# Gates of tiles 6 and 7 as seven block products, with attention's last steps between them

## The chip, the core and the metric

The kernel runs on one core of a Trainium2 chip. The metric is device time in microseconds, the median of several executions. The core has five engines with a queue each: TensorE (PE) multiplies, VectorE (DVE) and ScalarE (ACT) do element-wise work, GpSimd (POOL) does a little element-wise work here, and SyncE (SP) issues the DMAs. Each queue runs in program order; the queues meet only where one waits for another's result or for a buffer.

## What is computed

One decoder block on 512 tokens of width 1024, in float32. Its core, cut down:

```python
u = modulate(rmsnorm(h, g_norm_ffn1), sh1, sc1)
h = h + 0.5 * gt1 * swiglu(u, w_ffn1_in, w_ffn1_out)
u = modulate(rmsnorm(h, g_norm_mix), sh2, sc2)
proj = u @ w_in                       # p | q | k | v | gate_logits
y_pool = multiscale_pool(p, w_pool, pool_scale)
# rotary q, k; three groups of heads, dilations 1, 4, 16; groups joined by their softmax denominators
y_attn = einsum('gbsh,gbshd->bshd', softmax(lses), outs)
g_pool, g_attn = split(sigmoid(gate_logits), 2)
merged = g_pool * (y_pool @ w_pool_branch) + g_attn * (y_attn @ w_attn_branch)
h = h + gt2 * (merged @ w_out)
u = modulate(rmsnorm(h, g_norm_ffn2), sh3, sc3)
h = h + 0.5 * gt3 * swiglu(u, w_ffn2_in, w_ffn2_out)
return rmsnorm(h, g_final)
```

The nine modulation vectors (sh1 to gt3) are products of silu(c) with a 1024 x 9216 matrix, 72 rows of 128 results.

## The kernel before

Activations lie transposed, 128 features on the partitions and 512 tokens along them; a feature tile is 128 features, so there are 8 of them. Every float32 factor is split in a high and a low part (fp32r), and a product is three matmuls: high by high, high by low, low by high.

**Weights.** `plan` (L176) writes down the order in which PE consumes weights: `order` has one entry for each piece of 1024 columns, with the raw loads that it needs and, for block products, the sum that makes it. `fetch` issues loads from SP into three raw buffers as they come free. `split_hi` (ACT) and `split_lo` (DVE) write the high and low parts into a ring of 6784 columns; `make` (DVE, L313) forms a sum of raw blocks first where an entry asks for one. `look(n)` splits up to n entries ahead of the one PE is at, as far as the ring has room; `take` hands the parts to PE.

**Plain tiles and block products.** `mm_tile` computes one feature tile of `u @ w` with 8 x 3 matmuls of 512 columns. `gate_duo` (L1774) computes two gates of two feature tiles (four tiles' worth) by seven block products instead of eight: both factors are cut in 2 x 2 blocks, seven products of sums of blocks are formed, and the results are added. `product` (L741) is one of them, 24 matmuls of 256 columns. A `settle` matmul of 240 columns, whose result is overwritten, stands ahead of the first. The seven products need four sums of blocks of the weights (`make`) and four of u (`mix_sums`, L1310: each is formed on DVE and then split on ACT and DVE).

**The stage around the change.** `mix` (L1602) computes q, k, v and p, rope, and three attention groups. Attention is cut into units whose steps are hung between matmuls of other tiles as hooks at k = 0 to 7: `at_scores` (PE), `at_exp` (DVE, ACT), `at_turn` (PE transpose, ACT copy), `at_values` (PE, DVE copy). The loop over c = 0 to 3 (L1740) computes v of the two dilated groups for one class of tokens at a time; it needs a copy of u's high part sorted by class, which `by_class` (L1706, an ACT instruction) makes one pass ahead. Beside it run steps of `mix_sums` (`nxt`), the four weight pieces of v are all held in the ring, and POOL forms the pooling differences (`pool_diff`, L1560). Then come four plain gate tiles (L1756 to L1768, feature tiles 6 and 7, two gates each) with attention's last steps hung between them: the last `at_values`, `at_merge` (small DVE and ACT steps that weigh the groups), `pool_map`, `at_fT`, `at_spread` (PE) and `at_y` (DVE). `merge_out` (L1814) follows: the two branch products of tiles 6 and 7 with those gates, then three times a `gate_duo` and two branches, then the output product.

The background step `bg` (L466) computes one modulation row: a 512 KB load by SP and a 1024-wide DVE instruction (L449). Rows 45 to 59 belong to this stage.

Of the kernel before, what the change touches and what calls it, by code (L numbers as in the profile page):

```python
# [14 lines left out]
P = 128  # L15
# [146 lines left out]
def chunk_widths():  # L162
    outs = [D] * (KT // 2 * (len(PARTS) - 1)) + [(FT - PARTS[-1][0]) * P] * KT
    f1 = [2 * FIRST * P] * KT + [D] * (2 * (FT - FIRST)), outs
    mix = [D] * 24 + [4 * P] * 2 + ([D] * 4 + [4 * P] * 2) * (KT // 2 - 1) + [D] * KT
    return f1, mix, ([D] * (2 * FT), outs)


class Kernel:
# [6 lines left out]
    def plan(self):  # L176
# [1133 lines left out]
    def mix_sums(self, x, slots):  # L1310
# [13 lines left out]
        def lo(i):  # L1324
            L[i] = slots[i][1]()
            v.tensor_tensor(L[i], x[i], H[i], op=OP.subtract)

        sub = lambda o, y, z: v.tensor_tensor(o, y, z, op=OP.subtract)

        def last():  # L1330
# [3 lines left out]
            self.S[:3] = [[H[i], L[i]] for i in range(3)]  # L1334
# [4 lines left out]
                lambda: (hi(0), whole(x[3], 4, 0)), lambda: lo(0), lambda: (hi(1), sub(x[3], x[3], x[1])),  # L1339
                lambda: hi(2), lambda: lo(2), lambda: lo(1)], last  # L1340
# [219 lines left out]
    def pool_diff(self, t, bank):  # L1560
# [6 lines left out]
        d = self.kt[0][:, T * t:T * t + T]  # L1567
# [34 lines left out]
    def mix(self):  # L1602
# [12 lines left out]
        with tc.tile_pool(name="rt", bufs=1) as self.rt, tc.tile_pool(name="aw", bufs=2) as self.aw, \  # L1615
# [23 lines left out]
            self.ada_free, self.ada_stop, self.ada_depth = list(x), 57, 2  # L1639
# [15 lines left out]
            for n in range(4):  # L1655
# [15 lines left out]
                for _ in range((0, 0, 1, 2)[n]):  # L1671
# [42 lines left out]
            assert self.ada_next == 57 and not self.adat, self.ada_next  # L1714
            self.ada_free, self.ada_stop, self.ada_depth = [self.AR], 60, 1
            self.bg_fetch()
            v4 = []

            def half(i):
                if not v4:  # L1720
# [4 lines left out]
                                       [wide(ma, "v1"), wide(ma, "k0")], [lambda: half(0), lambda: half(1)]])  # L1725
            nxt = lambda: sums.pop(0)()
            b = self.mm_tile(hooks(g23[0], [(2, lambda: by_class(1)), (3, nxt)]))
# [4 lines left out]
            def clear():  # L1732
# [5 lines left out]
            beside = [(1, 7, nxt), (2, 2, nxt), (2, 3, clear), (2, 6, self.bg), (2, 7, nxt), (3, 2, self.at_swap), (3, 2, nxt),  # L1738
                      (3, 3, nxt), (3, 6, nxt), (3, 7, self.bg)]
# [19 lines left out]
            rest = [b for b in self.banks if b not in gates] + [self.bS[0]]  # L1759
            spread = [self.bS[1], self.bO] + self.bT  # L1760
            self.banks, self.bi = gates + rest + spread, 2

            at = [t[:, i * T:(i + 1) * T] for t in (self.qt[1], self.kt[1]) for i in range(2)]
            sig = lambda i: lambda: nc.scalar.activation(at[i], gates[i], AF.Sigmoid)
            gates.append(self.mm_tile({1: [nxt, sig(0)], 2: [sig(1)], 4: [lambda: self.at_spread(spread)]}))
            self.YH, self.YL = two("YH"), two("YL")
            self.at_y(spread)
            gates.append(self.mm_tile({1: [sig(2)]}))  # L1768
            sig(3)()
            assert not sums  # L1770
        self.merge_out(at, last, ma)
        outer.close()

    def gate_duo(self, s, c, p5, last, rest):  # L1774
# [11 lines left out]
        for i, (bank, u, start) in enumerate(((A, lambda: blk(lo4, T1), True), (B, lambda: S(0), True),  # L1786
# [8 lines left out]
            self.product(bank, u(), start, not i)  # L1795
# [13 lines left out]
            elif i == 6:  # L1809
                sig(q(s, 1), r(A))  # L1810
                v.tensor_tensor(q(c, 0), r(B), q(c, 0), op=OP.add)
        sig(c, c)

    def merge_out(self, ready, last, ma):  # L1814
        nc, tc = self.nc, self.tc
        v = nc.vector
        with tc.tile_pool(name="mg", bufs=1) as mg:
# [15 lines left out]
            def branch(m):  # L1833
# [16 lines left out]
                def parts():  # L1850
                    if m > 5:
                        place(tile_of(ma, ("q1", "k1")[m % 2]), m)
# [9 lines left out]
            for j in MERGED[::2]:  # L1862
# [6 lines left out]
                for m in (j, j + 1):  # L1869
                    if m < 4:  # L1870
                        place(tile_of(*((ma, "q0"), (ma, "o1"), (mg, "m3"), (ma, "q2"))[m]), m)
# [281 lines left out]
```

## Time and profile before

| what | value |
|---|---|
| median of 3 runs | 971.73 us (970.31 to 972.13) |
| profiled execution, own time | 970.52 us |
| its span | 968.7 us |
| PE, DVE, ACT, POOL busy | 99%, 88%, 56%, 8% |
| granted TensorE clock | 0.998 |
| loop over the classes of v, first to last matmul of 512 columns | 449.42 to 482.60 us |
| four plain gate tiles | 482.60 to 509.22 us |

The span lies inside the profiled execution's own time. Times in rows below are from the span's start. In a row of the timeline the first two numbers are start and duration; what stands in brackets is the idle time of the engine before it and who ended it. A row with "x2" holds two instructions. PE's durations overlap: a matmul lasts longer than the distance to the next one, and the distance is what it costs.

### The profile page before, as it was taken

To read this page: it belongs to the slowest core of one execution; us is meant where nothing else is said; L and a number is where in the kernel's file an instruction comes from. 1 tells how busy PE (TensorE), PEld (TensorE's weight loads), DVE (VectorE), ACT (ScalarE), POOL (GpSimd) and SP (SyncE) were. 2 spreads that over 40 slices of the span, in tenths; PEclk is the share of its full clock that TensorE was granted. 3 is DMA by queue.
4 is the path that set the end of the run, shared out by engine and by line. 5 is a ranking of instruction groups with operands and counts; after the bars stand their busy time and mean duration, and the time that the engine had idled before them with its cause. 6 is when DMAs were issued, how large, how long until landed. Compare 5 with 4: busy or idle time off the path is not lost.

```text
span 968.7 us, 17985 instructions
## 1 busy us (share of the span) xinstructions
PE 958.6 (99%) x7222; PEld 899.6 (93%) x7222; DVE 847.8 (88%) x1250; ACT 542.1 (56%) x823; POOL 72.9 (8%) x81
## 2 busy tenths in 40 slices
PE   8999999999999999999999999999999999999997
PEld 7888999999999899888879998998999999999996
DVE  7989999899999788897888877889898888989885
ACT  5443656665755553446545553465665747566555
POOL 0000110101010000006300000000101100110002
PEclk9999999999999999999999999999999999999999
DMA  9857786786768547664143327723757666665632
GB/s 349 287 174 261 192 238 161 197 217 153 204 185 260 163 145 209 225 194 157 40 137 112 107 66 238 242 68 113 189 147 192 163 171 169 161 171 137 172 76 88
DMA packets 51702, 167.81 MB, mean 173 GB/s; under 512 B 6945, under 2 KB 9761, under 8 KB 51618
## 3 DMA queue, kind: packets, MB, share of 16 engines
q1 hardware_dynamic: 43840, 140.18, 44.3%
q0 software_dynamic: 7200, 25.96, 14.9%
q8 instruction: 56, 0.92, 0.4%
q10 hardware_dynamic: 578, 0.53, 0.2%
q14 instruction: 28, 0.23, 0.1%
HBM read 135.29 MB, written 2.24 MB: 142 GB/s over the span
## 4 chain that ended last, share of the span: by engine, by line
PE 95%; DVE 2%; DMA 1%; issue 1%; POOL 0%; ACT 0%; SPq 0%; POOLq 0%; DVEq 0%
PE bank L751 13%; PE bank L750 13%; PE bank L752 13%; PE bank L422 10%; PE bank L424 10%; PE bank L423 10%; PE bank L1109 5%; PE bank L1110 5%; PE bank L1111 5%; PE bank L2079 2%; PE bank L2083 1%; PE bank L2081 1%; PE bank L1451 1%; PE bank L1748 1%; PE bank L1502 1%; PE bank L1749 1%
## 5 line engine op out<-in xcount | busy, mean ns | idle before, releaser
L390 DVE TENSOR_TENSOR wlo<-raw,whi 128x1024 fp32r<-128x1024 f32 (+6 forms) x157 | 166.7, 1074 | 33.0 <-ACT whi L378 32.7
L750 PE MATMUL bank<-UH,whi 128*128 128x256 f32 x640 | 176.7, 276 | 0.0
L751 PE MATMUL bank<-UL,whi 128*128 128x256 f32 x640 | 176.7, 276 | 0.0
L752 PE MATMUL bank<-UH,wlo 128*128 128x256 f32 x640 | 176.7, 276 | 0.0
L390 DVE TENSOR_TENSOR wlo<-X,whi 128x1024 fp32r<-128x1024 f32 (+6 forms) x140 | 142.8, 1034 | 17.5 <-ACT whi L378 17.4
L378 ACT ACTIVATE whi<-raw 128x1024 fp32r<-128x1024 f32 (+6 forms) x157 | 144.0, 934 | 23.9 <-DVE raw L313 10.4
L378 ACT ACTIVATE whi<-X 128x1024 fp32r<-128x1024 f32 (+6 forms) x140 | 123.7, 908 | 49.5 <-DVE X L313 45.5
L750 PEld LDWEIGHTS bank<-UH,whi 128*128 128x128 f32 x640 | 120.1, 188 | 0.2
L751 PEld LDWEIGHTS bank<-UL,whi 128*128 128x128 f32 x640 | 120.2, 188 | 0.0
L752 PEld LDWEIGHTS bank<-UH,wlo 128*128 128x128 f32 x640 | 120.2, 188 | 0.0
L750 PE MATMUL bank<-SH,whi 128*128 128x256 f32 x408 | 112.7, 276 | 0.0
L751 PE MATMUL bank<-SL,whi 128*128 128x256 f32 x408 | 112.6, 276 | 0.0
L752 PE MATMUL bank<-SH,wlo 128*128 128x256 f32 x408 | 112.6, 276 | 0.0
L422 PE MATMUL bank<-UH,whi 128*128 128x512 f32 (+1 forms) x304 | 105.9, 348 | 0.0
L423 PE MATMUL bank<-UL,whi 128*128 128x512 f32 (+1 forms) x304 | 104.5, 344 | 0.1
L424 PE MATMUL bank<-UH,wlo 128*128 128x512 f32 (+1 forms) x304 | 104.3, 343 | 0.0
L750 PEld LDWEIGHTS bank<-SH,whi 128*128 128x128 f32 x408 | 76.6, 188 | 0.0
L751 PEld LDWEIGHTS bank<-SL,whi 128*128 128x128 f32 x408 | 76.6, 188 | 0.0
L752 PEld LDWEIGHTS bank<-SH,wlo 128*128 128x128 f32 x408 | 76.6, 188 | 0.0
L422 PEld LDWEIGHTS bank<-UH,whi 128*128 128x128 f32 x304 | 57.1, 188 | 8.5 <-issue 1.9
L424 PEld LDWEIGHTS bank<-UH,wlo 128*128 128x128 f32 x304 | 57.3, 188 | 7.0
L423 PEld LDWEIGHTS bank<-UL,whi 128*128 128x128 f32 x304 | 57.1, 188 | 6.8 <-DVE UL L560 0.3
(421 smaller groups left out, 2401.3 us busy)
## 6 DMA issues: line engine op xcount, KB each, us to landing
raw<-wmix SPq DMA_DIRECT2D x44, 512.0 KB, 3.8
raw<-wf1i SPq DMA_DIRECT2D x32, 512.0 KB, 5.4
raw<-wf2i SPq DMA_DIRECT2D x30, 512.0 KB, 4.4
ada<-wada SPq DMA_DIRECT2D x23, 512.0 KB, 5.3
X<-raw POOLq DMA_DIRECT2D x23, 512.0 KB, 5.7
X<-wf2i SPq DMA_DIRECT2D x14, 512.0 KB, 5.1
AR<-wada SPq DMA_DIRECT2D x11, 512.0 KB, 4.2
X<-wf1i SPq DMA_DIRECT2D x11, 512.0 KB, 4.4
```

The costliest lines, as they stand in the source:

```text
L378: self.nc.scalar.activation(self.hi[:, y], r[:, x], AF.Copy)
L390: self.nc.vector.tensor_tensor(self.lo[:, y], r[:, x], self.hi[:, y], op=OP.subtract)
L422: M(ps, hi, uh, start=start, stop=False)
L423: M(ps, hi, ul, start=False, stop=False)
L424: M(ps, lo, uh, start=False, stop=stop)
L750: M(o, hi, uh, start=start and p == 0 and k == 0, stop=False, skip_group_check=True)
L751: M(o, hi, ul, start=False, stop=False, skip_group_check=True)
L752: M(o, lo, uh, start=False, stop=k == 3, skip_group_check=True)
L1109: M(o, hi, uh, start=start and m % 2 == 0 and k == 0, stop=False, skip_group_check=True)
L1110: M(o, hi, ul, start=False, stop=False, skip_group_check=True)
L1111: M(o, lo, uh, start=False, stop=k == 1, skip_group_check=True)
L2079: M(b, hi, self.UH[k], start=k == 0, stop=False)
```

## The change

The gates of tiles 6 and 7 become a fourth `gate_duo`, called from `mix` ahead of `merge_out`. It gets two dictionaries: `beside` (a function to call behind product 0, 1, 2 and 3) and `settles` (the bank for the settle matmul ahead of products 3 and 4). Behind product 0 stand the last `at_values`, `at_merge` and a sum's split; behind product 1 two more splits (`last` among them); behind product 2 `pool_map` and `at_fT`; behind product 3 `at_spread` and `at_y`. The weights' layout and `plan` follow. The steps of `mix_sums` are taken sooner: nine in the loop over c instead of six, and `begin` lets `make` start in pass c = 1, so that pass 1 ends with an entry that is a sum. Modulation rows 57, 58 and 59 are done in the v and k stage, in the buffers of the rows before them, instead of in `AR` beside the loop and the gates. The pooling difference is kept in `ev` instead of `k0`, and some tiles take each other's place.

```diff
--- before.py
+++ after.py
@@ lay_mix, chunk_widths, plan @@
-    for m in MERGED[:2]:
-        for base in GATES:
-            ch.append(_fmajor(w_in, base + np.arange(m * P, (m + 1) * P)))
     for j in MERGED[::2]:
-        if j < KT - 2:
-            ch.extend(_blocks(w_in, *GATES, j))
+        ch.extend(_blocks(w_in, *GATES, j))
...
-    mix = [D] * 24 + [4 * P] * 2 + ([D] * 4 + [4 * P] * 2) * (KT // 2 - 1) + [D] * KT
+    mix = [D] * 20 + ([D] * 4 + [4 * P] * 2) * (KT // 2) + [D] * KT
...
-        plain(mx[:26])
-        for i in range(26, len(mx) - KT, 6):
+        plain(mx[:20])
+        for i in range(20, len(mx) - KT, 6):
@@ product @@
-    def product(self, bank, u, start, extra=0):
+    def product(self, bank, u, start, extra=0, other=None):
...
-            self.settle(bank, w[0][0], self.UH[0])
+            self.settle(other if other is not None else bank, w[0][0], self.UH[0])
@@ mix_sums @@
-                lambda: (hi(0), whole(x[3], 4, 0)), lambda: lo(0), lambda: (hi(1), sub(x[3], x[3], x[1])),
-                lambda: hi(2), lambda: lo(2), lambda: lo(1)], last
+                lambda: (hi(0), whole(x[3], 4, 0)), lambda: lo(0), lambda: hi(1), lambda: sub(x[3], x[3], x[1]),
+                lambda: lo(1), lambda: hi(2), lambda: lo(2)], last
@@ pool_diff @@
-        d = self.kt[0][:, T * t:T * t + T]
+        d = self.ev[:, T * t:T * t + T]
@@ mix @@
-            self.ada_free, self.ada_stop, self.ada_depth = list(x), 57, 2
+            self.ada_free, self.ada_stop, self.ada_depth = list(x), 60, 2
...
-                for _ in range((0, 0, 1, 2)[n]):
+                for _ in range((0, 1, 1, 2)[n]):
                     self.bg()
...
-                        b = self.mm_tile(hooks(todo.pop(0), rest + [(7, self.bg)]))
+                        more = [(2, self.bg)] if g == 2 and dst is self.kt[2] else []
+                        b = self.mm_tile(hooks(todo.pop(0), rest + more + [(7, self.bg)]))
...
-            self.ada_free, self.ada_stop, self.ada_depth = [self.AR], 60, 1
-            self.bg_fetch()
...
+            self.X, self.retired = [self.AR, self.cs], []
+
+            def begin():
+                self.ready = True
...
-            beside = [(1, 7, nxt), (2, 2, nxt), (2, 3, clear), (2, 6, self.bg), (2, 7, nxt), (3, 2, self.at_swap), (3, 2, nxt),
-                      (3, 3, nxt), (3, 6, nxt), (3, 7, self.bg)]
+            beside = [(0, 2, nxt), (0, 7, nxt), (1, 2, nxt), (1, 3, nxt), (1, 3, begin), (1, 7, nxt), (2, 3, clear), (2, 7, nxt),
+                      (3, 1, nxt), (3, 2, self.at_swap), (3, 3, nxt), (3, 6, nxt)]
...
-            gates = [self.mm_tile(hooks([], [(2, nxt), (5, self.at_merge), (7, nxt)]))]
-            pool_map = lambda: self.pool_map(two("PH"), two("PL"))
-            gates.append(self.mm_tile({1: [self.bg, nxt], 3: [nxt], 6: [pool_map, lambda: self.at_fT(self.bS[1])]}))
...
-            gates.append(self.mm_tile({1: [nxt, sig(0)], 2: [sig(1)], 4: [lambda: self.at_spread(spread)]}))
-            self.YH, self.YL = two("YH"), two("YL")
-            self.at_y(spread)
-            gates.append(self.mm_tile({1: [sig(2)]}))
-            sig(3)()
+            nxt()
+            values = hooks([])[5]
+            spread = [self.bS[1], self.bO] + self.bT
...
+            def first():
+                for f in values:
+                    f()
+                self.at_merge()
+                nxt()
+
+            def third():
+                self.pool_map(two("PH"), two("PL"))
+                self.at_fT(self.bS[1])
+
+            def fourth():
+                self.at_spread(spread)
+                self.YH, self.YL = two("YH"), two("YL")
+                self.at_y(spread)
+
+            self.gate_duo(self.qt[1], self.kt[1], self.ev[:, 2 * T:3 * T], None, lambda n=1: None,
+                          {0: first, 1: lambda: (nxt(), last()), 2: third, 3: fourth}, {3: self.bT[0], 4: self.bS[0]})
...
-        self.merge_out(at, last, ma)
+        self.merge_out(at, None, ma)
@@ gate_duo @@
-    def gate_duo(self, s, c, p5, last, rest):
+    def gate_duo(self, s, c, p5, last, rest, beside={}, settles={}):
...
-            self.product(bank, u(), start, not i)
+            self.product(bank, u(), start, not i or i - 1 in beside and i != 2, settles.get(i))
...
+            if i in beside:
+                beside[i]()
```

More of the change, by code (lines that the diff above doesn't have):

```diff
@@ L1326, in lo @@
             v.tensor_tensor(L[i], x[i], H[i], op=OP.subtract)
+            self.S[i] = [H[i], L[i]]
         sub = lambda o, y, z: v.tensor_tensor(o, y, z, op=OP.subtract)
@@ L1713, in mix @@
             self.pool_diff(0, b)
-            assert self.ada_next == 57 and not self.adat, self.ada_next
-            self.ada_free, self.ada_stop, self.ada_depth = [self.AR], 60, 1
-            self.bg_fetch()
+            assert self.ada_next == 60 and not self.adat, self.ada_next
             v4 = []
@@ L1755, in mix @@
             self.held = None
[L1756 to L1759 removed]
+            nxt()
+            values = hooks([])[5]
             spread = [self.bS[1], self.bO] + self.bT
[L1761 to L1769 removed]
+            banks = list(self.banks)
+            def first():
[12 more added lines that the diff above has]
+                          {0: first, 1: lambda: (nxt(), last()), 2: third, 3: fourth}, {3: self.bT[0], 4: self.bS[0]})
             assert not sums
[L1771 removed]
+            at = [t[:, i * T:(i + 1) * T] for i in range(2) for t in (self.qt[1], self.kt[1])]
+            self.banks, self.bi = [self.bS[0]] + spread + banks, 0
+        self.merge_out(at, None, ma)
         outer.close()
[L1774 removed]
+    def gate_duo(self, s, c, p5, last, rest, beside={}, settles={}):
         nc, v = self.nc, self.nc.vector
@@ L1851, in parts @@
                     if m > 5:
-                        place(tile_of(ma, ("q1", "k1")[m % 2]), m)
+                        place(tile_of(ma, ("q2", "k1")[m % 2]), m)
                     nc.scalar.activation(MH[m], gp, AF.Copy)
@@ L1870, in merge_out @@
                     if m < 4:
-                        place(tile_of(*((ma, "q0"), (ma, "o1"), (mg, "m3"), (ma, "q2"))[m]), m)
+                        place(tile_of(*((ma, "q0"), (ma, "o1"), (mg, "m3"), (ma, "q1"))[m]), m)
                     elif m == 4:
```

3 lines of the change are left out of this document (1 added, 2 removed).

## The prediction

> **What bounds the kernel now.** I read the page first, then the stretches of the stage by time, then PE's timeline.
>
> ```profile
> span 968.7 us, 17985 instructions
> PE 95%; DVE 2%; DMA 1%; issue 1%; POOL 0%; ACT 0%; SPq 0%; POOLq 0%; DVEq 0%
> 353.00:386.00 33.00, 33.00 (x269) 32.02 (x269) 28.07 (x47) 14.41 (x24) 0.00 (x0) 1.00 0.71 221
> 446.20:482.60 36.40, 36.40 (x251) 31.12 (x250) 26.86 (x61) 21.16 (x49) 21.12 (x18) 1.00 0.23 69
> 482.60:509.20 26.60, 26.60 (x133) 20.14 (x132) 22.55 (x38) 11.79 (x19) 0.00 (x0) 1.00 0.41 129
> ```
>
> PE is 95% of the chain that ended last. In the three stretches, v of the first group, the loop over the classes and the gates (columns: length, then busy time of PE, PE's loads, DVE, ACT, POOL, clock, DMA), it never idles, so time falls only if PE gets less to do, and rises if PE has to wait. DVE is busy 22.55 of 26.60 us in the gate stretch: the engine that an added wait will come from.
>
> **PE's saving.** The distance of matmuls in a gate tile (first and last of tile 4's 24), and a whole gate_duo, from its settle to the branch behind it (the last row is from the chain):
>
> ```profile
> 503.78 0.39 PE L422 MATMUL bank<-UH,whi 128*128 128x512 f32 x1
> 509.00 0.39 PE L424 MATMUL bank<-UH,wlo 128*128 128x512 f32 x1
> 514.66 0.27 PE L428 MATMUL bank<-UH,whi 128*128 128x240 f32 x1
> 514.77 0.28 PE L750 MATMUL bank<-UH,whi 128*128 128x256 f32 x1
> 533.99 0.23 PE bank L422
> ```
>
> (509.00-503.78)/23 = 0.227 us; four tiles are 96 of them, 21.8 us. Seven products are 168 matmuls in 533.99-514.77 = 19.2 us, 0.1144 each, 2.75 a product. The call has settles ahead of products 0, 1, 3 and 4, at 0.11 each: 0.4. So PE is relieved of 21.8-19.2-0.4 = **2.1 us**. Attention's steps interrupt PE three times before and after, so their own PE time is counted at nothing; should a short matmul behind an interruption cost as much extra as a long one, that is in both sums.
>
> **What DVE and ACT get instead.** Seven ring entries in place of four (three more splits on each engine), four weight sums on DVE, two DVE additions and three ACT copies of results. Three of DVE's modulation rows leave this stretch. What these cost PE depends on where an instruction that PE waits for stands in DVE's and ACT's queues. There are two such places.
>
> **Place 1: the sorted copy for pass 2.** PE's pass 2 begins at 466.07 and needs by_class's copy, an ACT instruction behind the transposes' copies and behind the split of whatever entry the loop makes in pass 1.
>
> ```profile
> 462.51 1.08 ACT L1487 ACTIVATE probT<-bank 128x512 f32<-128x512 f32 x2 [3.23 <-PE bank L1484]
> 463.48 2.07 ACT L1709 ACTIVATE uc<-UH 128x1024 fp32r<-128x1024 f32 x1
> 466.07 0.40 PE L1748 MATMUL bank<-whi,uc 128*128 128x512 f32 x1
> 458.23 1.05 ACT L378 ACTIVATE whi<-raw 128x1024 fp32r<-128x1024 f32 x1
> 452.27 2.39 DVE L390 TENSOR_TENSOR wlo<-raw,whi 128x1024 fp32r<-128x1024 f32 x2 [2.70 <-ACT whi L378]
> 455.07 0.43 DVE L1467 CUSTOM_DVE_ANT_0 prob<-bank,masks 128x256 f32<-128x256 f32 x1 [0.41 <-PE bank L1451]
> 456.76 0.38 DVE L1469 TENSOR_SCALAR negmax<-st 128x2 f32<-128x2 f32 x1
> 457.36 0.69 DVE L1754 COPY v<-bank 128x512 f32<-128x512 f32 x1 [0.22 <-PE bank L1750]
> ```
>
> The copy ends at 465.55, 0.5 ahead. Pass 1's split by ACT (458.23) reads a raw load. In the changed kernel it reads a weight sum, so ACT stops until DVE has made it, with the transposes' copies and by_class queued behind; by_class is what PE waits for. Ahead of that sum DVE now has, from 452.27: v's last low part, a step of u's sums, a low part, the exp group (1.85 us from the rows at 455.07 and 456.76), a step, the copy of v (0.6), two steps, the sum. An instruction over 128x1024 comes every 1.14 us (half of what the x2 row lasts, less its tail). That is 452.27 + 7 x 1.14 + 1.85 + 0.6 = 462.7; ACT's split +1.0, transposes' copies +1.0, by_class +2.05 = 466.8. PE would wait **0.7 us** if nothing slows DVE.
>
> But POOL works until 468.42, and the rows show that it and DVE hold each other up:
>
> ```profile
> 444.49 1.30 DVE L390 TENSOR_TENSOR wlo<-raw,whi 128x1024 fp32r<-128x1024 f32 x1 [0.82 <-ACT whi L378]
> 444.78 1.93 POOL L1575 TENSOR_TENSOR rt<-rt 64x525 f32<-64x525 f32 x1
> 445.71 2.08 DVE L1318 TENSOR_TENSOR cs<-UH,UL 128x1024 f32<-128x1024 f32 x1
> 452.31 1.27 POOL L1583 TENSOR_TENSOR k<-rt,cst 64x16 f32<-64x16 f32 x1
> 449.11 0.21 POOL L1583 TENSOR_TENSOR k<-rt,cst 64x16 f32<-64x16 f32 x1
> 457.19 1.06 POOL L1575 TENSOR_TENSOR rt<-rt 128x525 f32<-128x525 f32 x1
> 467.12 1.30 POOL L1584 TENSOR_TENSOR k<-k,v 64x512 f32<-64x512 f32 x1
> 467.48 2.02 DVE L1337 TENSOR_TENSOR PH<-PH,cs 128x1024 f32<-128x1024 f32 x1
> ```
>
> POOL's operation asked at 444.78, while DVE's ran; 1.06 is its undisturbed length (457.19), so at 1.93 it started when DVE's ended, 445.65. DVE's next, asked at 445.71, took 2.08 instead of the 1.2 that one of the two at 452.27 lasts: it ran when POOL's had ended, 446.71. The same at 467.12 and 467.48 (DVE waits until 468.42), and at 452.31, where 0.21 became 1.27. So two-input operations go one at a time, and in a dense DVE queue a waiting POOL operation gets in between. The exp group and the copy of v, which read PSUM, are not held (455.07 has its usual length), and POOL gets on meanwhile. Walking both queues with these lengths, DVE's waits are 0.2 (first step), 1.3 (low part), 0.35 and 0.45 (two steps), 1.05 (third): 3.35 us. Place 1 then costs 0.7+3.35 = **4.1 us**. If moreover the two added modulation rows of the k tiles delay the start, there is more:
>
> ```profile
> 435.18 0.69 DVE L1413 TENSOR_TENSOR rt<-rt,cs 128x512 f32<-128x512 f32 x1 [0.70 <-DMA rt<-tr]
> 442.59 1.08 DVE L1414 TENSOR_TENSOR k<-k,rt 128x512 f32<-128x512 f32 x1
> 446.15 1.16 PE L1451 MATMUL bank<-k,q 64*128 64x128 f32 x16
> 447.72 0.41 DVE L1467 CUSTOM_DVE_ANT_0 prob<-bank,masks 128x256 f32<-128x256 f32 x1
> ```
>
> 2 x 1.14, less the 0.7 idle at 435.18, puts k's rope (442.59) 1.6 later; it ends 445.2, still ahead of the scores at 446.15, but now falls under POOL's first two operations and pushes the first exp group from 447.72 to about 449.4, 1.6 us. Bounds of place 1: 0.7 and 4.1+1.6 = 5.7. I take 4.1: the hold-ups have rows, the late start is only worked out.
>
> [...]
>
> **Place 2: the spreading of the weights.** Before, these were the rows:
>
> ```profile
> 486.13 1.10 PE L1502 MATMUL bank<-probT,v 128*64 128x128 f32 x16
> 487.28 0.61 DVE L1507 COPY q<-bank 128x256 f32<-128x256 f32 x1 [0.39 <-PE bank L1502]
> 489.39 1.22 DVE L1328 TENSOR_TENSOR q<-q,YL 128x1024 f32<-128x1024 f32 x1
> 493.51 1.09 PE L1595 MATMUL bank<-k,wpool 64*64 64x512 f32 x8
> 495.45 1.41 DVE L1600 SCALAR_TENSOR_TENSOR PL<-bank,vecs,PH 128x512 fp32r<-128x512 f32 x2 [1.97 <-ACT PH L1599]
> 495.50 0.50 PE L422 MATMUL bank<-UH,whi 128*128 128x512 f32 x1
> 496.89 0.68 DVE L1540 TENSOR_TENSOR fT<-bank,fT 8x512 fp32r<-8x512 f32 x1
> 499.80 1.20 PE L1546 MATMUL bank<-fT,sel 64*128 64x512 f32 x4
> ```
>
> at_spread (499.80) needs fT, done at 497.57: 2.2 to spare, and DVE idle 1.97 ahead of 495.45. After the change, counted from the end of pass 3: PE reaches at_spread after four products (11.0), three settles (0.35), values (1.1), pool_map and at_fT (495.50-493.51 = 2.0), some 0.1 extra at each of two interruptions: 14.7. DVE can start lo1 only when pass 3 has ended, because the low part takes the buffer of the sorted copy. Its queue up to fT: copy of v 0.8, lo1, two low parts with a sum and a third low part (five at 1.14: 5.7), o's copy and at_merge (489.39-487.28 = 2.1), then sum, low part, lo2, last's low part, low part (5.7), PL 1.4, fT 0.7: 16.4.  PE waits 16.4-14.7 = **1.7 us**. Bounds: 0, if two of the ten come early, and 4.0, if hi2 or a split by ACT holds DVE for two more.
>
> **What is hidden.** The rest of the gate_duo's additions lie behind at_y, beside the branches, with the first gate_duo of merge_out rid of last (1.14 on DVE); splits run four entries ahead, so PE has about 10 us of cover, and if that is gone it costs what DVE lags. The raw loads and at_swap keep their places in SP's queue, and the loads for pass 1's sum have had a pass to land, beside 3.8 us in the page's row for wmix. The three modulation rows' loads move with them, ahead of ropes on SP; each is issued two rows before its use, over 6 us ahead, beside 5.3 to land. The row added to v of the first group meets 4.9 us of idle DVE in that stretch (33.00-28.07) and costs nothing; without that cover it would cost its 1.14:
>
> ```profile
> raw<-wmix SPq DMA_DIRECT2D x44, 512.0 KB, 3.8
> ada<-wada SPq DMA_DIRECT2D x23, 512.0 KB, 5.3
> ```
>
> A row that landed late would cost its delay on DVE, and through k's rope as much on PE.
>
> **Sum.** -2.1 + 4.1 + 1.7 = +3.7 us. The profiled execution's own time is 970.52 us (span 968.7), the median of the runs 971.73. From 970.52 it is 974.2, from the median 975.4; I take the middle of the two, 971.1, as base: **974.8 us**.
>
> **Rivals.**
>
> *Faster: DVE's idle time takes it all, 969.0.* One mechanism: the added instructions fall into idle stretches, so no queue is late at either place. For it: in pass 0 and 1 the rows show idle times of 2.70, 0.41 and 0.22 on DVE, PE has waited nowhere in this stage, and place 1 misses by only 0.7 without POOL. Against it: the 2.70 comes before v's low part, where the added steps can't go. It decides if DVE has pass 1's sum by 462.0 and fT by 14.7 after pass 3: 971.1-2.1 = 969.0. Chance 0.30.
>
> *No change: POOL doesn't hold the steps.* Place 1 costs 0.7, place 2 1.7: +0.3, 971.4. For it: DVE's low part at 452.27 lost hardly anything to POOL (2.39 for two). Chance 0.18.
>
> *Slower still: the late start comes too.* Place 1 at 5.7: +5.3, 976.4. Chance 0.17; against it, before the change the first exp group started the moment that DVE was free, and ACT absorbs part.
>
> **How the numbers follow.** The forecast has 0.35. About 0.2% (1.9 us) is what a measurement of this kernel can tell from no change. Faster 0.30, same 0.18, slower 0.35+0.17 = 0.52. The range reaches from the faster case to the worst with 0.9 for the runs' spread above: 968.8 to 977.3; the forecast's own range goes from place 2 at 0 (973.1) to the slower rival (976.4).
>
> **What would show it.** Place 1: idle PE at the first matmul of pass 2, named for the sorted copy, and ACT's split in pass 1 waiting for a DVE sum. Hold-ups: steps of u's sums lasting about 2 us in passes 0 and 1. Place 2: at_spread waiting for fT. PE's saving: the call from its first settle to the branch, less these waits, about 2 us shorter than 26.6. I am wrong if pass 2 starts without idle time on PE, or if fT is ahead of at_spread.

## The result, and the profile after

The changed kernel takes 980.95 us (median of 4 runs, 979.84 to 982.43), the kernel before 971.02 beside it: ratio 1.0105, interval 1.0082 to 1.0128. It is **slower by 9.9 us** where 3.7 were forecast. The direction and both places are as forecast; the size is not: three things that the sum put at nothing cost time too, the late start of the loop over the classes, the modulation row beside v, and the `gate_duo`'s last additions. The profiled execution took 982.43 us itself.

The page, its span and its chain, and then the answer on what PE waited for (us in total, times, longest):

```profile
span 980.6 us, 18125 instructions
...
PE 73%; DVE 14%; DMA 5%; issue 4%; ACT 3%; SPq 1%; POOL 0%; POOLq 0%; DVEq 0%; ACTq 0%
```

```profile
PE bank L1748 <- ACT uc L1706: 3.0, 1, 3.0
PE bank L1498 <- DVE v L1754: 3.0, 1, 3.0
PE bank L1542 <- DVE fT L1536: 1.6, 1, 1.6
PE bank L746 <- ACT bank L1787: 1.1, 1, 1.1
...
PE bank L1749 <- DVE wlo L386: 0.8, 1, 0.8
```

PE's share of the chain falls from 95% to 73%; DVE's rises to 14%. The waits are for the sorted copy of pass 2 (place 1), for DVE's copy of v in pass 1 (not forecast), for fT at the spreading (place 2), for a copy by ACT in the first `gate_duo` of `merge_out` (not forecast), and for v's last low part in pass 0.

Four stretches hold nearly all of it. Before, and after (each: from the first scores of the first group to the scores of class 0; the loop over the classes; the gates of tiles 6 and 7 with their branches, up to the first settle of `merge_out`'s first `gate_duo`; that `gate_duo` with its branches):

```profile
385.32:446.15 60.83, 60.83 (x334) 48.61 (x333) 54.43 (x104) 29.61 (x63) 2.54 (x3) 1.00 0.64 207
446.15:482.60 36.45, 36.45 (x251) 31.17 (x250) 26.91 (x61) 21.21 (x49) 21.17 (x18) 1.00 0.23 69
482.60:514.66 32.06, 32.06 (x157) 24.64 (x156) 26.51 (x43) 15.24 (x23) 0.00 (x0) 1.00 0.40 123
514.66:539.29 24.63, 24.63 (x194) 23.67 (x193) 21.22 (x25) 14.53 (x20) 0.00 (x0) 1.00 0.33 108
```

```profile
384.64:447.58 62.94, 62.17 (x334) 48.59 (x333) 57.48 (x109) 29.37 (x63) 1.79 (x3) 1.00 0.68 219
447.58:493.35 45.77, 39.02 (x250) 32.13 (x250) 35.94 (x64) 22.92 (x51) 23.57 (x18) 0.96 0.12 36
493.35:524.83 31.48, 29.91 (x233) 26.71 (x232) 28.07 (x41) 18.01 (x27) 0.00 (x0) 1.00 0.37 114
524.83:551.36 26.53, 25.43 (x194) 24.27 (x193) 22.67 (x28) 14.72 (x21) 0.00 (x0) 1.00 0.30 104
```

In each row the first number behind the stretch is its length; then come the busy times of PE, PE's weight loads, DVE, ACT and POOL, the granted clock, and DMA. That is +2.1, +9.3, -0.6 and +1.9 us, 12.7 together; the spans differ by 11.9, so the rest of the kernel was 0.8 shorter in this execution. The loop is the loss, and it is DVE's: its busy time (the third of the busy times) goes from 26.91 to 35.94 us for three instructions more.

**The loop, read in DVE's and POOL's rows.** DVE, POOL and ACT in passes 0 and 1:

```profile
446.33 1.83 DVE L1410 TENSOR_TENSOR k<-k,rt 128x512 f32<-128x512 f32 x1
448.07 2.11 DVE L386 TENSOR_TENSOR wlo<-raw,whi 128x1024 fp32r<-128x1024 f32 x1
450.10 1.61 DVE L1314 TENSOR_TENSOR cs<-UH,UL 128x1024 f32<-128x1024 f32 x1
451.64 0.41 DVE L1463 CUSTOM_DVE_ANT_0 prob<-bank,masks 128x256 f32<-128x256 f32 x1
451.87 1.29 POOL L1580 TENSOR_TENSOR ev<-ev,tr 64x512 f32<-64x512 f32 x1
452.44 0.75 DVE L1465 TENSOR_SCALAR negmax<-st 128x2 f32<-128x2 f32 x1
456.76 1.96 DVE L386 TENSOR_TENSOR wlo<-raw,whi 128x1024 fp32r<-128x1024 f32 x1 [2.69 <-ACT whi L374]
457.71 6.16 POOL L1571 TENSOR_TENSOR rt<-rt 128x525 f32<-128x525 f32 x3
458.64 2.08 DVE L1314 TENSOR_TENSOR PH<-UH,UL 128x1024 f32<-128x1024 f32 x1
460.64 2.07 DVE L386 TENSOR_TENSOR wlo<-raw,whi 128x1024 fp32r<-128x1024 f32 x1
465.83 0.68 DVE L1754 COPY v<-bank 128x512 f32<-128x512 f32 x1
466.43 1.98 DVE L1314 TENSOR_TENSOR YL<-UH,UL 128x1024 f32<-128x1024 f32 x1
469.87 1.24 DVE L309 TENSOR_TENSOR AR<-raw,raw 128x1024 f32<-128x1024 f32 x1
471.14 1.06 ACT L374 ACTIVATE whi<-AR 128x1024 fp32r<-128x1024 f32 x1 [5.06 <-DVE AR L309]
473.06 2.04 ACT L1706 ACTIVATE uc<-UH 128x1024 fp32r<-128x1024 f32 x1
475.15 0.50 PE L1748 MATMUL bank<-whi,uc 128*128 128x512 f32 x1 [2.98 <-ACT uc L1706]
```

Between 456.76 and 462.7, DVE and POOL change turns: three additions of POOL take 6.16 us beside three of DVE at some 2 us each, where 1.22 is DVE's undisturbed length (the row of e2_no_pool below). The copy of v comes behind them, at 465.83, and PE's `at_values` stands waiting for it. The weight sum comes at 469.87, so ACT's split has waited 5.06 us, and the transposes' copies and `by_class` follow one after the other. This is the chain of place 1, only longer.

### The profile page after: what moved, and what is told of

It reads as the page before. It is cut to its first block, busy times and chain, and to the rows that moved or that the text cites. A ratio compares the mean times of both kernels' runs of the same rounds, so it can differ in the third digit from the quotient of the medians.

```text
span 980.6 us, 18125 instructions
## 1 busy us (share of the span) xinstructions
PE 960.7 (98%) x7298; PEld 902.3 (92%) x7298; DVE 860.7 (88%) x1248; ACT 545.6 (56%) x818; POOL 74.6 (8%) x81
## 4 chain that ended last, share of the span: by engine, by line
PE 73%; DVE 14%; DMA 5%; issue 4%; ACT 3%; SPq 1%; POOL 0%; POOLq 0%; DVEq 0%; ACTq 0%
PE bank L746 12%; PE bank L747 11%; PE bank L748 11%; PE bank L419 6%; PE bank L418 6%; PE bank L420 6%; PE bank L1105 4%; PE bank L1107 4%; PE bank L1106 4%; DVE wlo L386 3%; PE bank L2091 2%; PE bank L2093 1%; PE bank L2095 1%; SPq L1390 1%; DMA cs<-wada 1%
## 5 line engine op out<-in xcount | busy, mean ns | idle before, releaser
L386 DVE TENSOR_TENSOR wlo<-raw,whi 128x1024 fp32r<-128x1024 f32 (+3 forms) x152 | 168.7, 1120 | 32.2 <-ACT whi L374 31.8
L374 ACT ACTIVATE whi<-raw 128x1024 fp32r<-128x1024 f32 (+3 forms) x152 | 143.7, 958 | 30.9 <-DVE raw L309 14.0
L386 DVE TENSOR_TENSOR wlo<-X,whi 128x1024 fp32r<-128x1024 f32 (+3 forms) x133 | 142.2, 1081 | 17.3 <-ACT whi L374 17.1
L374 ACT ACTIVATE whi<-X 128x1024 fp32r<-128x1024 f32 (+3 forms) x133 | 123.0, 946 | 50.3 <-DVE X L309 45.8
L746 PEld LDWEIGHTS bank<-UH,whi 128*128 128x128 f32 x672 | 126.3, 188 | 0.2
L747 PEld LDWEIGHTS bank<-UL,whi 128*128 128x128 f32 x672 | 126.2, 188 | 0.0
L748 PEld LDWEIGHTS bank<-UH,wlo 128*128 128x128 f32 x672 | 126.1, 188 | 0.0
L1105 PE MATMUL bank<-HI,whi 128*128 128x256 f32 x224 | 61.8, 276 | 0.0
L1106 PE MATMUL bank<-HK,whi 128*128 128x256 f32 x224 | 61.8, 276 | 0.0
L1107 PE MATMUL bank<-HI,wlo 128*128 128x256 f32 x224 | 61.8, 276 | 0.0
```

The lines of the kernel that those rows point to most:

```text
L374: self.nc.scalar.activation(self.hi[:, y], r[:, x], AF.Copy)
L386: self.nc.vector.tensor_tensor(self.lo[:, y], r[:, x], self.hi[:, y], op=OP.subtract)
L746: M(o, hi, uh, start=start and p == 0 and k == 0, stop=False, skip_group_check=True)
L747: M(o, hi, ul, start=False, stop=False, skip_group_check=True)
L748: M(o, lo, uh, start=False, stop=k == 3, skip_group_check=True)
L1105: M(o, hi, uh, start=start and m % 2 == 0 and k == 0, stop=False, skip_group_check=True)
```

## The experiments

All medians are of several runs; the kernel before had 970.7 to 971.0 us beside them. The table gives the four stretches of the profiled execution of each, measured as above. Two of the kernels leave POOL's part out, and e12_less_dve leaves out attention's second group; their outputs lack it.

| kernel | median us | ratio and interval | v and k | loop | gates | first gate_duo |
|---|---|---|---|---|---|---|
| before | 971.0 | 1 | 60.83 | 36.45 | 32.06 | 24.63 |
| changed | 980.95 | 1.0105 (1.0082 to 1.0128) | 62.94 | 45.77 | 31.48 | 26.53 |
| e1_rows | 981.97 | 1.0112 (1.0096 to 1.0127) | 61.31 | 42.45 | 31.51 | 26.14 |
| e2_no_pool | 975.28 | 1.0045 (1.0033 to 1.0058) | 61.63 | 37.83 | 33.32 | 24.62 |
| e3_begin | 980.66 | 1.0103 (1.0089 to 1.0117) | 62.41 | 41.73 | 35.68 | 24.63 |
| e4_spread | 980.33 | 1.0106 (1.0088 to 1.0125) | 62.01 | 44.12 | 29.86 | 27.43 |
| e5_row1 | 980.39 | 1.0094 (1.0081 to 1.0107) | 60.88 | 44.03 | 33.13 | 24.62 |
| e6_late | 976.54 | 1.0057 (1.0044 to 1.0070) | 62.31 | 39.88 | 31.80 | 26.04 |
| e7_fill | 981.31 | 1.0104 (1.0091 to 1.0117) | 62.20 | 44.11 | 31.48 | 25.94 |
| e8_all | 975.79 | 1.0048 (1.0035 to 1.0061) | 60.84 | 39.65 | 29.86 | 29.11 |
| e10_spots | 975.55 | 1.0047 (1.0030 to 1.0064) | 62.63 | 37.98 | 29.86 | 28.68 |
| e12_less_dve | 971.91 | 1.0010 (1.0000 to 1.0019) | 61.78 | 38.15 | 29.86 | 25.22 |
| e11_rows_only | 972.36 | 1.0015 (1.0007 to 1.0024) | 62.46 | 37.96 | 32.06 | 24.63 |
| e13_before_no_pool | 970.59 | 1.0000 (0.9991 to 1.0008) | 60.87 | 36.49 | 32.05 | 24.63 |

### POOL's share

```diff
@@ pool_diff: e2_no_pool, e13_before_no_pool @@
-        (the chain of shifted additions)
+        g.memset(d, 0.0)
```

> The changed kernel without the pooling sums: POOL only fills the result with zeros, so the pooling branch's values are missing. Theory A (POOL's two-input operations hold DVE's up, 0.8 us a time): DVE's steps of 1.8 to 2.1 us in passes 0 and 1 fall to 1.2, some 5 us in sum up to the copy of v, so PE's wait for that copy (3.0) goes to nothing and that for the sorted copy (3.0) to under 1; the stretch at half clock goes too; 972 to 975 us. Theory B (the queue is simply too long): the waits stay above 2 us each and the time within 2 us of 981.

> The kernel before the change without POOL's chain of additions for the pooled branch (its values are missing in the output, as in the changed kernel without it). Theory A (POOL's hold-ups cost time only where DVE's queue is dense, as the change makes it): 970.5 to 971.5, no gain. Rival B (POOL holds DVE up in any case, and the gain of 5.7 us in the changed kernel is not the change's): 966 to 968.

Without POOL's chain the changed kernel is 5.7 us faster, just short of the expected 972 to 975; the kernel before gains nothing (0.2 us, within its interval). The loops of the two, changed and before (the second window ends 0.04 us ahead of the loop's end):

```profile
447.73:485.56 37.83, 36.73 (x250) 31.16 (x250) 28.59 (x63) 22.84 (x51) 0.00 (x0) 1.00 0.15 44
```

```profile
444.89:481.34 36.45, 36.45 (x250) 31.16 (x250) 24.96 (x61) 21.03 (x49) 0.00 (x0) 1.00 0.22 67
```

In the changed kernel DVE's busy time in the loop falls from 35.94 to 28.59: 7.4 us of hold-ups. Before, it falls from 26.91 to 24.96, 2.0 us, and that costs PE nothing because the queue has idle time. The same sum, alone and beside POOL:

```profile
455.49 1.22 DVE L1314 TENSOR_TENSOR PH<-UH,UL 128x1024 f32<-128x1024 f32 x1
```

1.22 us here, 2.08 at 458.64 above. So the hold-ups that cost time are the change's doing: it puts DVE's steps where POOL works, in a queue without idle time. And in these kernels the queues of DVE and POOL meet also where neither waits for the other's result or for a buffer.

### The start of the weights' sums, and u's sums

```diff
@@ e3_begin @@
-            (1, 3, begin), (1, 7, nxt), (2, 3, clear), (2, 7, nxt),
+            (1, 7, nxt), (2, 3, clear), (2, 7, nxt), (2, 7, begin),
@@ e6_late @@
-            (0, 2, nxt), (0, 7, nxt), (1, 2, nxt), (1, 3, nxt), (1, 3, begin), (1, 7, nxt), (2, 3, clear), (2, 7, nxt),
+            (1, 2, nxt), (1, 7, nxt), (2, 2, nxt), (2, 3, nxt), (2, 3, begin), (2, 3, clear), (2, 6, nxt), (2, 7, nxt),
```

> The changed kernel with the first weight sum allowed only behind pass 2, so that ACT splits it in pass 3. Theory A (ACT stops for the sum, with the sorted copy behind it): PE's wait of 3.0 us at pass 2 is gone, and with it the 3.4 us at half clock (1.7 us); the wait for the copy of v in pass 1 stays at 3.0, since it lies ahead of the sum on DVE; 975 to 977 us. Theory B (the lateness only moves on, because DVE has the same work): another wait takes its place in pass 3 or the gates, and the time stays within 1.5 us of 981.

> u's sums go back to about where they were before: none of them in pass 0, two in pass 1, four in pass 2; the point from which weights are summed moves from pass 1 to pass 2. All else as in the changed kernel. Theory A (the early sums are late because DVE is dense in passes 0 and 1 while POOL works, and DVE has idle time in passes 2 and 3 to take them): PE's waits for v and for the sorted copy, 3.0 each, and the half clock behind them, 1.7, are gone, and 973 to 975 is left. Rival B (DVE's work up to the spreading is one sum, so that what is put off is missing there): the two waits are gone but the wait for fT grows from 1.6 to 5 or more, 978 to 981.

Moving the start alone gives 980.66, no gain. Place 1's wait is gone, and the loop is 4.0 us shorter, but the sums are now missing later:

```profile
PE bank L1498 <- DVE v L1754: 3.0, 1, 3.0
PE bank L1542 <- DVE fT L1536: 2.4, 1, 2.4
```

The gates take 35.68 instead of 31.48. Of these 4.2 us the longer wait is 0.8; two periods at half clock follow it (0.90 is the clock of the stretch), in which PE's busy time grows by 3.3. The mechanism of place 1 is confirmed, and its removal pays nothing. Putting u's sums off as well gives 976.54: 4.4 us less than the changed kernel. The wait for v goes, 1.6 for the sorted copy (of pass 3 now) and 0.8 for v's low part stay, and the wait for fT doesn't grow (1.6), as theory A had it. The expected 973 to 975 was not reached.

### The spreading one product later

```diff
@@ e4_spread @@
-                          {0: first, 1: lambda: (nxt(), last()), 2: third, 3: fourth}, {3: self.bT[0], 4: self.bS[0]})
+                          {0: first, 1: lambda: (nxt(), last()), 2: third, 4: fourth}, {3: self.bT[0], 5: self.bS[0]})
```

> The changed kernel with at_spread and at_y behind product 4 instead of product 3. Theory A (place 2: fT is 1.6 us late for product 3): that wait is gone, nothing takes its place since at_y still ends ahead of the branches; 1.0 to 1.8 us less than the changed kernel, 979 to 980. Theory B (at_y then comes late for the branches): PE waits at the branches for 1 us or more, and the time stays at 981.

The wait for fT is gone, and the stretch of the gates takes 29.86 without any idle PE, **2.2 us less** than the four plain tiles did. This is PE's saving, seen bare. But the next wait, in the first `gate_duo` of `merge_out`, grows from 1.1 to 2.2 us, and that stretch from 26.53 to 27.43. Neither theory had a wait at that place. The median gains 0.6 us, within the intervals.

### The modulation rows

```diff
@@ e1_rows: rows 57 to 59 beside the output product, 15 there @@
-                for _ in range((0, 1, 1, 2)[n]):
+                for _ in range((0, 0, 1, 2)[n]):
...
-                        b = self.mm_tile(hooks(todo.pop(0), rest + more + [(7, self.bg)]))
+                        b = self.mm_tile(hooks(todo.pop(0), rest + [(7, self.bg)]))
...
-            for _ in range((2, 2, 3, 2, 1)[m]):
+            for _ in range((2, 3, 3, 2, 1)[m]):
@@ e5_row1: the row of n = 1 beside the second q tile of the next group @@
-                for _ in range((0, 1, 1, 2)[n]):
+                for _ in range((0, 0, 1, 2)[n]):
...
-                        more = [(2, self.bg)] if g == 2 and dst is self.kt[2] else []
+                        more = [(2, self.bg)] if g == 2 and dst is self.kt[2] or (g, hp) == (1, 1) and dst is self.qt[1] else []
```

> The changed kernel with rows 57 to 59 taken out of the v and k stage and done beside the output product instead (15 rows there for 12). Theory A (DVE enters the loop late, and the rows' 3 x 1.14 us are part of why): the first transposes, which start PE's next tile 1.6 us late in the changed kernel, are on time again, the first exp group of the loop starts about 2 us nearer to its scores, and PE's two waits of 3.0 us in passes 1 and 2 shrink to 1 to 2 each; 974 to 977 us beside the changed kernel's 981. Theory B (the row's cover in the v stage holds, only the crowd in passes 0 and 1 counts): the first transposes stay late or were late for another reason, and the time falls by less than 1.5 us. Either way the output product may lose up to 1 us.

> The one modulation row that the change adds beside v of the first group (n = 1) is computed beside the second q tile of the next group instead, where DVE stands idle for 2.7 us; the other two rows and all else stay as in the changed kernel. Theory A (this row alone pushes the first exp group by 1.7 us, and with it the transposes, so that all of the stage is 1.4 us late): the wait for prob at the first transposes is gone, the scores of class 0 come 1.4 us earlier, 979 to 979.6. Rival B (the stage has slack, what it is late is taken up again before the loop over the classes): 980.5 to 981.5.

> The kernel before the change with one part of it alone: the three modulation rows computed beside v of the first group and the k tiles, as the changed kernel has them, and no longer in the class loop and beside the gates. Theory A (the row beside v makes the stage 2 us late, and nothing takes that up): 972.8 to 974. Rival B (the stage's lateness is taken up in the class loop, or the rows that the later stages lose give it back): 970.5 to 971.8.

In the changed kernel, these are the rows around the added one (a modulation row, the low part behind it, the start of the exp group, PE's transposes, the next rope):

```profile
388.01 1.22 DVE L445 SCALAR_TENSOR_TENSOR PH<-PH,cond 128x1024 f32<-128x1024 f32 x1
389.15 1.22 DVE L386 TENSOR_TENSOR wlo<-raw,whi 128x1024 fp32r<-128x1024 f32 x1
390.29 0.28 DVE L1463 CUSTOM_DVE_ANT_0 prob<-bank,masks 128x128 f32<-128x128 f32 x1
391.57 1.49 PE L1480 MATMUL bank<-cst,prob 128*128 128x128 f32 x4 [0.55 <-ACT prob L1468]
398.21 0.69 DVE L1409 TENSOR_TENSOR rt<-rt,cs 128x512 f32<-128x512 f32 x1 [2.71 <-DMA rt<-tr]
```

DVE is dense up to the exp group and idle behind it: 2.71 us ahead of 398.21. The four transposes take 1.49 us, with each waiting for its own probabilities; before, they took 0.60. In e5_row1 the row stands in that idle time, and the stretch takes 60.88 us, as before the change (60.83). So the row beside v costs 2.1 us of this stretch here, and 1.2 to 2.1 over the six executions that have it there and POOL's chain (62.01 to 62.94 us). Its removal moved the median by only 0.6 us, within the intervals: the loop stayed at 44 us, and the gates lost 1.7 to a period at half clock (33.13, clock 0.95).

With the kernel before, the rows alone cost 1.6 us in the median (972.36, a little under the expected 972.8 to 974): 1.6 in the stretch of v and k, and 1.5 in the loop, of which 0.8 is the wait for v's last low part. The stretches together give more than the medians; this one execution was 1.1 shorter ahead of them, where the edit changes nothing.

**The rows beside the k tiles.** e1_rows takes these two away as well, and its loop is shorter: 42.45 us, where e5_row1, which leaves them, has 44.03. In e1_rows these are the last rope of k, the first exp group of the loop (in the changed kernel they stand at 446.33 and 451.64), the whole loop, and a period in it:

```profile
443.64 1.11 DVE L1410 TENSOR_TENSOR k<-k,rt 128x512 f32<-128x512 f32 x1
448.69 0.41 DVE L1463 CUSTOM_DVE_ANT_0 prob<-bank,masks 128x256 f32<-128x256 f32 x1
446.64:489.09 42.45, 38.36 (x250) 32.21 (x250) 33.51 (x63) 23.24 (x51) 25.52 (x18) 0.96 0.13 39
471.92:475.33 3.41, 3.41 (x10) 2.64 (x9) 3.32 (x8) 2.00 (x8) 1.29 (x1) 0.50 0.00 0
```

The first exp group starts 4.1 us behind the scores of class 0 in the changed kernel, 2.05 in e1_rows and 1.6 in the kernel before. With the rows, k's rope comes later, falls beside POOL's additions and lasts 1.83 instead of 1.1; v's low part and a step of u's sums, held in both kernels, follow it. In all eight executions that have these two rows and POOL's chain, e11_rows_only among them, the group starts 3.7 to 4.1 behind the scores; without the chain (e2_no_pool) 2.1. So the loop starts late because of the rows and POOL together. (In e10_spots and e12_less_dve below the rows stand in earlier tiles, and the group still starts 3.5 to 3.6 behind. Why was not followed up.)

The late start costs at least the 1.6 us by which the two loops differ, and 1.5 in e11_rows_only, where the sums are as before. The loop of e1_rows also has a period at half clock behind its last wait (the last row), which the 44.0 to 44.1 us don't contain: PE is busy for 38.36 us, 1.6 more than in e2_no_pool at full clock. Taken off, this gives an estimate of 40.9 for e1_rows, and of 3.2 us for the late start.

The median of e1_rows doesn't show this, because the rows cost at the output product what they save here (5.3 us over the four stretches):

```profile
PE bank L424 <- DVE H L1917: 3.3, 1, 3.3
```

```profile
622.11:625.52 3.41, 1.24 (x6) 0.70 (x4) 2.69 (x4) 0.00 (x0) 0.00 (x0) 1.00 1.01 345
625.52:632.35 6.83, 5.74 (x27) 5.77 (x28) 6.79 (x12) 2.66 (x4) 0.00 (x0) 0.50 0.79 266
```

PE waits 3.3 us there for the residual, and 6.8 us at half clock follow (the 0.50 in the second row). DMA is busy all through the wait (1.01). So the median of this run doesn't tell the theories apart, but its trace does: theory A's late start is there. The two waits didn't both shrink: that for v fell to 0.5, that for the sorted copy rose to 3.6.

### The half clock

```diff
@@ e7_fill, ahead of pass 2, and the same ahead of pass 1's at_values @@
+                    for _ in range(12):
+                        M(b, uc[1][:, :P], w[0][0], start=True, stop=True, skip_group_check=True)
```

> Twelve matmuls whose result nobody reads stand in front of each of the two waits of 3.0 us (for v in pass 1 and for the sorted copy in pass 2); all else as in the changed kernel. They take 2.7 us of time in which PE stood idle. Theory A (a period in which PE does little is followed by 3.4 us at half clock, which costs another 1.7 us): no stretch at half clock behind these waits, 979.0 to 979.6. Rival B (the half clock costs nothing, because DVE is late anyway and PE would wait for it further on): 980.5 to 981.5.

In the changed kernel the two periods before and behind pass 2's start are these (the clock is the third number from the end):

```profile
472.33:475.74 3.41, 0.59 (x3) 0.55 (x4) 3.38 (x9) 2.77 (x3) 0.00 (x0) 1.00 0.42 150
475.74:479.15 3.41, 3.41 (x10) 2.64 (x10) 3.33 (x10) 2.08 (x8) 0.00 (x0) 0.50 0.00 0
```

PE is busy 0.59 of 3.41 us, and the next 3.41 us run at half clock, ten matmuls where some fifteen fit. With the matmuls in the waits no half clock is left, and the loop takes 44.11 instead of 45.77, 1.7 us less, in the profiled execution. But the median is 981.31, as without them. In e4_spread and e5_row1 the half clock came behind the first wait, with the second still ahead, and there too the loop took 44.1 and 44.0 us: PE was slower and waited less afterwards. So, in these runs, the half clock costs only where it comes behind the last wait. How often that is in the executions without a trace is open; the median shows no cost.

### The remedies together, and DVE as the bound

e8_all has the edits of e5_row1, e6_late and e4_spread. e10_spots has e4_spread's edit and no row beside v of n = 1, and in place of the rest of the first two:

```diff
-                        more = [(2, self.bg)] if g == 2 and dst is self.kt[2] else []
+                        more = [(2, self.bg)] if (g, dst is self.kt[g], hp) in ((1, False, 1), (1, True, 0), (2, False, 0)) else []
...
-            (0, 2, nxt), (0, 7, nxt), (1, 2, nxt), (1, 3, nxt), (1, 3, begin), (1, 7, nxt), (2, 3, clear), (2, 7, nxt),
+            (1, 2, nxt), (1, 3, nxt), (1, 7, nxt), (2, 2, nxt), (2, 2, begin), (2, 6, nxt), (2, 7, nxt), (2, 7, clear),
```

and e12_less_dve is e10_spots without

```diff
-            v.tensor_tensor(y, y, banks[2 * hp + 1], op=OP.mult)
-            v.tensor_tensor(x, x, y, op=OP.add)
```

> The two above together (the row beside q, u's sums late) and the spreading behind the fifth product instead of the fourth. Theory A: no wait over 1 us between 385 and 530, so that PE's saving of 2 us is seen: 969 to 971.5. Rival B: as with the sums put off alone, 976 to 979.

> As in the run with all three remedies, but each in a better place: all three modulation rows stand beside tiles in which DVE idles (the second q tile and the first k tile of one group, the first q tile of the next), and u's sums go one step further ahead (three in pass 1, with the start of the weights' sums ahead of pass 2's split, and the clearing of fT behind them). Theory A (what is left in the loop over the classes, 3.2 us, is PE's wait of 0.7 for v's last low part and of 1.6 for pass 3's sorted copy, both of DVE's making): the loop costs at most 1 us more than before, 973 to 974.5. Rival B (DVE has so much to do from pass 1 to the branches that what it wins early it loses later): the waits are gone but those behind the gates grow, 975.5 to 977.

> As the one with all in better places, and attention's second group is left out of the output: of the steps behind the spreading DVE does four instructions of 128x512 less, 2.4 us. Theory A (behind pass 3 DVE is the bound up to the branches, and what it lacks shows as PE's wait in the first gate_duo of merge_out): that wait, and the half clock behind it, go, 2 us or more less than without this edit. Rival B (the wait there is ACT's, whose sigmoids and splits stand in a queue of their own): no more than 0.5 us less.

Both remedied kernels stay at 975.6 to 975.8 us: theory A's times were not reached. In e10_spots the loop costs 1.5 us more than before instead of 9.3, and the gates save 2.2, but the first `gate_duo` takes 28.68, 4.1 more than before. The stretch of v and k takes 62.63: the modulation rows are not free in the tiles where DVE idled either (61.78 in e12_less_dve, with the same rows). The gates and that `gate_duo`, in e10_spots and then in e12_less_dve:

```profile
484.57:514.43 29.86, 29.86 (x234) 26.73 (x232) 28.12 (x41) 16.95 (x26) 0.00 (x0) 1.00 0.32 100
514.43:543.11 28.68, 26.52 (x194) 25.37 (x193) 22.59 (x27) 15.78 (x22) 0.00 (x0) 0.94 0.36 117
```

```profile
484.19:514.05 29.86, 29.86 (x233) 26.73 (x232) 26.62 (x38) 19.29 (x28) 0.00 (x0) 1.00 0.39 124
514.05:539.27 25.22, 25.22 (x194) 24.26 (x193) 21.70 (x28) 13.48 (x19) 0.00 (x0) 1.00 0.32 105
```

In the gates DVE is busy 28.12 of 29.86 us (before: 26.51 of 32.06). Freed of 2.4 us of work, it lets the first `gate_duo` run without a wait, and the median falls by 3.6 us. This is more than the 2.2 us of the wait, because in e10_spots a period at half clock follows it (0.94 in its last row; PE's busy time is 1.3 longer than in e12_less_dve). The gain confirms that DVE is the bound behind pass 3. How it holds PE there, in e10_spots:

```profile
513.07 0.68 DVE L1821 TENSOR_TENSOR k<-bank,k 128x512 f32<-128x512 f32 x1
513.78 1.06 ACT L1795 ACTIVATE k<-k 128x1024 f32<-128x1024 f32 x1 [3.06 <-DVE k L1821]
515.83 1.23 DVE L386 TENSOR_TENSOR wlo<-cs,whi 128x1024 fp32r<-128x1024 f32 x1 [2.08 <-ACT whi L374]
520.20 1.06 ACT L374 ACTIVATE whi<-raw 128x1024 fp32r<-128x1024 f32 x1 [3.46 <-DVE raw L309]
521.68 0.58 ACT L1787 ACTIVATE bank<-bank 128x512 f32<-128x512 f32 x1
```

DVE's last addition for the gates is late, so ACT's last sigmoid waits, and ACT's split behind it; DVE then waits for the split. The next split waits for a weight sum, and the copy behind it, at 521.68, is what PE waits for. It is place 1's pattern once more. e12_less_dve leaves work out, so no version here is faster than the kernel before.

## Why the prediction was half right

**PE's saving, -2.1: right.** The gates without a wait take 29.86 instead of 32.06 in three of these kernels with all work done (2.2 us).

**Place 1, +4.1: right in place and mechanism, but the sum left out the late start.** The loop costs 9.3 more in the profiled execution of the changed kernel, and 7.6 in the three others with the sums early, the rows beside the k tiles and no half clock behind the last wait (44.0 to 44.1 us). The step that failed is "I take 4.1: the hold-ups have rows, the late start is only worked out". The late start came: the first exp group was 2.5 us later than before, counted from the scores, where 1.6 had been worked out, and it costs 1.6 us of the loop, about 3.2 by the estimate above. Without it, by the same estimate, the loop of e1_rows is some 4.4 above the kernel before, and 4.1 had been forecast for that. So the rival "late start" (chance 0.17), with its two rows beside the k tiles, named a real cause.

The term "3.35 us" for POOL's hold-ups was too small, in part for the same reason. With POOL's chain away the loop takes 37.83, so in the late queue POOL costs 44.1 less 37.83, 6.3 us. The walk found five held instructions; the trace shows ten. Missing were the rope of the last k tile (1.83 instead of 1.08), which comes with the late start, v's low part in pass 0 (2.11), and the small operation behind an exp group (0.75 for negmax instead of 0.17). The prediction's own row at 456.76 shows that operation held already (0.38), though it calls the exp group not held. Each hold-up puts the next steps deeper into the time in which POOL works. The term "0.7 without POOL" came out at 1.1 us of wait and 1.4 of the loop.

That PE would stop at DVE's copy of v in pass 1 was missed: I followed the queue to one wait, and not each of PE's needs along it. It adds little to the sum, since what is late there is not late again at pass 2: in e1_rows the wait for v is 0.5 instead of 3.0, and that for the sorted copy 3.6.

**Place 2, +1.7: right.** 1.6 us at the spreading, for fT.

**"The row added to v of the first group meets 4.9 us of idle DVE in that stretch and costs nothing": wrong.** It costs 1.2 to 2.1 us. The idle time was real, but it lay behind the exp group that the row delays. A stretch's idle sum doesn't say on which side of the deadline it lies.

**"The rest of the gate_duo's additions lie behind at_y, beside the branches": wrong.** They, and the low parts late with them, made DVE the bound up to the first `gate_duo` of `merge_out`, +1.9 us in the changed kernel and +4.1 to 4.5 where the earlier waits are cured; of these 2.2 are the wait, and most of the rest is the half clock behind it. The 10 us of cover, from splits that run four entries ahead, wasn't there: in these rows ACT and DVE hand each split to and fro without a lead.

With +2.1, +7.6, -0.6 and +1.9 the sum is +11.0, beside +9.9 in the medians and +11.9 in the profiled spans, where the loop has 1.7 more from the half clock. The prediction has no term for the half clock. The faster case fell with the hold-ups: DVE's idle time before pass 1 did not take the sums.

## What to carry to other kernels

Before giving a busy engine more work, sum it per stretch between two deadlines, not per stage: idle time helps only ahead of the instruction that someone waits for. Look in the trace for steps that last longer while another engine works (here DVE's additions of two tensors, 2.0 us instead of 1.2 beside POOL's chain), price the steps that move there at that length, and walk the queue again with each delay added. When an engine is at 94% of a stretch, curing one wait only shows the next; remove a piece of that engine's work as an experiment before moving its steps about.

## What was not expected of the hardware

In the changed kernel not only DVE's additions of two tensors last longer beside POOL's chain (2.08 us at 458.64, 1.22 without the chain) but also a small TENSOR_SCALAR (negmax, 0.75 us at 452.44; the next one, at 453.90, takes 0.17). Under way beside it was POOL's operation of 451.87, which ends at 453.16; negmax ends at 453.19.

Ahead of the kernel's end, the granted clock fell to half for 3.41 us, or twice that, behind each of nine periods of 3.41 us in which PE was busy for 17 to 43% (0.59 us in the row above), and also behind two of 54 and 56%; others of 44 to 54% were not followed by it. Three executions had it at two places, and the two starts lay a whole number of these lengths apart: 40.96 us or 12 of them in e3_begin (465.26 and 506.22), 44.37 or 13 in e5_row1 (464.88 and 509.25), 153.60 or 45 in e1_rows (471.92 and 625.52). Waits of one length were followed by it or not: that of 3.0 us for v had half clock behind it in e5_row1 (35% busy) and none in the changed kernel (47%), and that of 2.2 us in the first `gate_duo` had it in e10_spots (43%) and not in e4_spread (44%). From these rows the author's estimate is that what a wait costs depends on how it lies in that grid; no run varies that alone. The busy shares are as the profile models them.
